# Splitting a chunk's outputs over two visits of a recurrence chain, with its value transposes in the chain's own bank

## The chip, the cores and the metric

The kernel runs on one core of one Trainium2 chip. The metric is the device time of one execution in microseconds; the time before is the median of three runs.

## The reference, cut to what matters

One layer of a hybrid block on 512 tokens with 16 learned tokens in front (528), width 1024, all in float32:

```
u = rmsnorm(h); proj = u @ w_in
y_rw = rwkv7_branch(...)          # 8 heads of 64: S = S (diag(w) + a^T b) + v^T k ; y = S r
                                  # then a group norm per head, a bonus term, and a gate
y_fx = fox_branch(...)            # 8 heads of causal attention with a forget gate
h = h + (gA * (y_rw @ w_out_rw) + gB * (y_fx @ w_out_fx)) @ w_o
z = rmsnorm(h)
h = h + square(relu(z @ w_up)) @ w_down
```

The change touches the recurrence S, the group norm behind it, and the transposes of z.

## The kernel before, in words

**Products.** Big matrix products are made from a rounded part and a remainder of each factor, in three passes (`passes`). Every transpose is a TensorE (PE) instruction against an identity, from SBUF into PSUM, and ACT and DVE copy the result out.

**The recurrence.** The 8 heads form 4 pairs; a pair's two heads lie on partitions 0 to 63 and 64 to 127 (`hss`). Time is cut into 9 chunks of 64 tokens. Two chains (`chain(g, prs)`, g = 0 and 1) carry two pairs each through the chunks. A chunk has three visits, with a `yield` between them at which other work may come in:

1. L1053: products of the rows L with the state and the values `uv[:, 1]`, into part 0 of the bank `pch` (tag `ch`); DVE copies them to `Rs` (L1055).
2. The inverse visit, L1059: the inverse `Tt` times `Rs`, into part 1 of the same bank; two DVE copies (L1061), one for each half of the partitions, make u, `uv[:, 0]`. `new_uv` transposes the next chunk's values (L1039) into a bank of the tag `py`, and ACT copies them out (L1041). ACT also scales the old state (L1071).
3. L1076: the state's update into part 2 of `pch`, added by DVE (L1078). Then the chunk's outputs, from the second chunk on: four products with L (L1084) and four with Bm (L1087), in a bank of the tag `py`, copied out by ACT (L1088).

The tag `py` has one buffer, so that value transposes and outputs take it in turns; the tag `ch` has one too. Each product of float32 stands in the profile as two instructions, so four products are eight.

**The order.** PE's order in this stage is the order in which the program writes its instructions. `Turns.run` writes it: streams of work (the chains at rank 0, the preparation of the chains at 1, attention at 2 and 3, group norm at 4, projections at 8) yield a time at which they can go on, and the planner takes the first by rank whose time, by the planner's own model of the engines (`Clock`), has come. The model knows when tiles are written and when a bank is free for its next tile; it keeps no times for parts of a tile:

```
SLACK = 0.15
HOP = 0.15
RATE = {"DVE": (0.18, 1.06e-3), "Activation": (0.25, 0.85e-3), "Pool": (0.30, 2.1e-3)}
```

Projections (L580) are what is left to fill in; when all else is done the rest of them follows. The orders of ACT, DVE and the queues are made by the framework, and so are all waits between engines.

**Group norm.** `group_norm` takes four chunks of outputs, normalises them, and turns them with eight transposes of 128 rows and 64 columns (L1114), a bank for each pair; ACT copies them out (L1122) and DVE finishes (L1124, L1125). The gate's products are L1117.

**The MLP's rows.** After the merge, `turned(i, xt)` transposes 128 tokens of z: eight transposes of 128 by 128 (L1264) in two banks, each copied out by ACT (L1265) and DVE (L1266). It runs four times, between the groups of products L1274.

Attention does two things that the prediction uses: scores on half the rows each (L738), and transposed weights (L770) in one bank, from which DVE copies some columns (L773) and ACT others (L774). Key transposes are L947.

Of the kernel before, what the change touches and what calls it, by code (L numbers as in the profile page):

```python
# [9 lines left out]
F32 = mybir.dt.float32  # L10
# [4 lines left out]
ALU = mybir.AluOpType  # L15
# [11 lines left out]
KB = 8  # L27
# [160 lines left out]
def kernel(ctx, tc, ht, x, win, par, cst, gain, lora, wout, wo, wup, wdn, out, dbg=None):  # L188
    nc = tc.nc
    dbg = dbg or {}  # L190
    mm = nc.tensor.matmul
    act = nc.scalar.activation
    V, G, A = nc.vector, nc.gpsimd, nc.scalar
# [12 lines left out]
    ident, ones_blk, tmask, cmask = (cs[:, 128 * i:128 * i + 128] for i in range(4))  # L206
# [74 lines left out]
    ps = ctx.enter_context(tc.tile_pool(name="ps", bufs=2, space=PSUM))  # L281
# [4 lines left out]
    with ExitStack() as st:  # L286
# [5 lines left out]
        def psm(name="psm"):  # L292
            return ps.tile([128, 512], F32, name=name, tag="sm", bufs=4)
# [23 lines left out]
        ck = Clock(nc)  # L317
# [9 lines left out]
        with tc.tile_pool(name="xp", bufs=2) as xp:  # L327
            ones = xp.tile([128, 128], F32, name="ones", bufs=1)
            V.memset(ones, 1.0)
            xt = [yp.tile([128, KB, HT], F32, name=f"xt{t}", tag=("y_rw", "y_fx")[t]) for t in range(2)]  # L330
# [30 lines left out]
            def rest(i):  # L361
                V.tensor_tensor(olo[i], raws[i], ohi[i].bitcast(F32), ALU.subtract)
# [142 lines left out]
        turns = Turns(tc, ck)  # L505
        hss = [slice(0, 64), slice(64, 128)]
# [299 lines left out]
        def v9(t):  # L806
            return t.rearrange("p (a b) -> p a b", b=64)
# [218 lines left out]
        def chain(g, prs):  # L1026

            y = y_rw[:, 2 * g:2 * g + 2, :].rearrange("p a (b c) -> p a b c", c=64)
            lws = [load_lora(2 * g + pr_, 1, 2) for pr_ in range(2)]

            def ppy(name):
                return ps.tile([128, 512], F32, name=name, tag="py", bufs=1)

            def new_uv(c):

                uv = rp.tile([128, 2, 2, 2, 64], F32, name="uv", bufs=2)
                pv = ppy("pvt").rearrange("p (a b) -> p a b", b=128)
                for pr_ in range(2):
                    nc.tensor.transpose(pv[:64, pr_, :], prs[pr_].ov[:, 64 * c:64 * c + 64], ident)  # L1039
                for e in range(2):  # L1040
                    A.copy(uv[hss[1 - e], :, e, :, :], bc(pv[:64, :2, 64 * e:64 * e + 64], 1, 2))  # L1041
                return uv

            yield lambda: math.inf if lent else max(ck.ready(Tt, prs[1].bkT), ck.ring("py", 1, 1))
            uv = new_uv(0)
            for e, hs in enumerate(hss):
                V.memset(uv[hs, 1, e, :, :], 0.0)
            for c in range(NCH):
                yield lambda: max(ck.ready(uv), ck.ring("ch", 1, 1) if c == 0 else 0.0)
                ch = ps.tile([128, 512], F32, name="pch", tag="ch", bufs=1)[:, :384].rearrange("p (a b c) -> p a b c", b=2, c=64)  # L1050
                for pr_ in range(2):
                    for e, hs in enumerate(hss):
                        mm(ch[hs, 0, pr_, :], prs[pr_].L[e][:, c, :64], uv[:, 1, e, pr_, :], start=True, stop=True)  # L1053
                Rs = rp.tile([128, 2, 64], F32, name="Rs")
                V.tensor_copy(Rs, ch[:, 0])  # L1055
                yield lambda: ck.ready(Rs)
                for pr_ in range(2):
                    for hs in hss:
                        mm(ch[hs, 1, pr_, :], Tt[hs, pr_, c, :], Rs[hs, pr_], start=True, stop=True)  # L1059
                for e, hs in enumerate(hss):  # L1060
                    V.tensor_copy(uv[hs, 0, e], ch[hs, 1])  # L1061
                if c < NCH - 1:
                    nxt = new_uv(c + 1)
                    if c == NCH - 2:
                        values_read[g].done = True
                        if g == 0:
                            seconds[0].ask_values()
                    SP = rp.tile([128, 2, 64], F32, name="SP")
                    for e, hs in enumerate(hss):
                        for pr_ in range(2):  # L1070
                            act(SP[hs, pr_], uv[hs, 1, e, pr_], AF.Copy, scale=prs[pr_].pend[hs, c:c + 1])  # L1071
                yield lambda: max(ck.ready(uv), ck.ring("py", 1, 1))
                if c < NCH - 1:
                    for pr_ in range(2):
                        for e, hs in enumerate(hss):
                            mm(ch[hs, 2, pr_, :], prs[pr_].bkT[:, c, 64 * e:64 * e + 64], uv[:, 0, e, pr_, :], start=True, stop=True)  # L1076
                    for e, hs in enumerate(hss):
                        V.tensor_tensor(nxt[hs, 1, e], ch[hs, 2], SP[hs], ALU.add)  # L1078
                if c > 0:

                    py = v9(ppy("pyy"))
                    for pr_ in range(2):
                        for e, hs in enumerate(hss):
                            mm(py[hs, pr_, :], prs[pr_].L[e][:, c, 64:128], uv[:, 1, e, pr_, :], start=pr_ == 0, stop=False)  # L1084
                    for pr_ in range(2):
                        for e, hs in enumerate(hss):
                            mm(py[hs, pr_, :], prs[pr_].Bm[hs, c, 64:128], uv[hs, 0, e, pr_, :], start=False, stop=pr_ == 1)  # L1087
                    A.copy(y[:, :, c - 1, :], py[:, :2, :])  # L1088
                if c in (4, 8):
                    turns.add(4, group_norm(g, y[:, :, c - 4:c, :], c - 4, prs, lws))  # L1090
                if c < NCH - 1:
                    uv = nxt
            chained[g].done = True
            chains[0] -= 1

        def group_norm(g, y, c0, prs, lws):

            st1 = rp.tile([128, 2, 4], F32, name="st1")
            V.tensor_reduce(st1, y, AX.X, ALU.add)
            V.tensor_scalar(st1, st1, 1.0 / 64, None, ALU.mult)  # L1100
            V.tensor_tensor(y, y, bc(st1, 3, 64), ALU.subtract)
            ysq = rp.tile([128, 2, 4, 64], F32, name="ysq", tag="Ain")
            act(ysq, y, AF.Square)
            st2 = rp.tile([128, 2, 4], F32, name="st2")
            V.tensor_reduce(st2, ysq, AX.X, ALU.add)
            V.tensor_scalar(st2, st2, 1.0 / 64, 64e-5, ALU.mult, ALU.add)
            rs = rsqrt(st2, rp, "rsg", [128, 2, 4])
            V.tensor_tensor(y, y, bc(rs, 3, 64), ALU.mult)
            yield lambda: max(ck.ready(y_rw), banks(3))
            pts = [psm("pyt").rearrange("p (a b) -> p a b", b=128) for pr_ in range(2)]  # L1110
            pos = psm("pg").rearrange("p (a b) -> p a b", b=256)
            for pr_ in range(2):
                for i in range(4):
                    nc.tensor.transpose(pts[pr_][:64, i, :], y[:, pr_, i, :], ident)  # L1114
            for pr_ in range(2):
                for n, (a, b) in enumerate(passes(lws[pr_], [x[:, 1, NM + 64 * c0:NM + 64 * c0 + 256] for x in (lhi, llo)])):
                    mm(pos[:, pr_, :], a, b, start=n == 0, stop=n == 2)  # L1117
            for pr_ in range(2):
                p = 2 * g + pr_
                yT = rp.tile([128, 4, 64], F32, name="yT", bufs=1)  # L1120
                for e, hs in enumerate(hss):
                    A.copy(yT[hs], pts[pr_][:64, :, 64 * e:64 * e + 64])  # L1122
                yf = yT.rearrange("p a b -> p (a b)")
                V.scalar_tensor_tensor(yf, yf, pr[:, C_LG + p:C_LG + p + 1], prs[pr_].bv[:, 64 * c0:64 * c0 + 256], ALU.mult, ALU.add)  # L1124
                V.tensor_tensor(y_rw[:, p, 64 * c0:64 * c0 + 256], yf, pos[:, pr_, :], ALU.mult)  # L1125
            normalised[g][c0 // 4].done = True
# [64 lines left out]
    def ppd():  # L1191
        tag = ("pj", "pj", "ch", "py")[wide[0] % 4]
        wide[0] += 1
        return ps.tile([128, 512], F32, name="pd", tag=tag, bufs=2 if tag == "pj" else 1)

    with ExitStack() as st:
# [42 lines left out]
        for b2 in range(4):  # L1239
            w = load_w(wo[0, b2])  # L1240
            for i, b1 in [(i, b1) for b1 in range(2) for i in range(4)] if b2 < 3 else [(i, b1) for i in range(4) for b1 in range(2)]:
                k = 2 * b2 + b1
# [13 lines left out]
            act(xt[:, :512], hr, AF.Square, accum_out=ssb[:, i:i + 1])  # L1256
            V.tensor_scalar(ssb[:, i:i + 1], ssb[:, i:i + 1], 1.0 / 1024, 1e-6, ALU.mult, ALU.add)
        def turned(i, xt):
            tk = slice(128 * i, 128 * i + 128)
            for j in range(2):  # L1260
                kk = slice(4 * j, 4 * j + 4)
                pt = ppd().rearrange("p (b c) -> p b c", c=128)
                for k in range(4):
                    nc.tensor.transpose(pt[:, k, :], xt[:, 512 * j + 128 * k:512 * j + 128 * k + 128], ident)  # L1264
                A.copy(zhi[:, kk, tk], pt)  # L1265
                V.tensor_tensor(zlo[:, kk, tk], pt, zhi[:, kk, tk].bitcast(F32), ALU.subtract)  # L1266

        normed = []
        for i in range(4):
# [291 lines left out]
```

## Time and profile before

| | us |
|---|---|
| median of three runs | 840.73 (839.65 to 841.92) |
| profiled execution, its own time | 840.95 |
| span of its instructions | 839.2 |
| PE busy / PE weight loads | 826.2 / 679.4 |
| DVE / ACT / POOL busy | 606.9 / 451.9 / 117.8 |
| first chain, from its first product (L1053) to its last inverse product (L1059) | 135.0 to 193.4 |
| second chain, the same | 300.2 to 350.5 |

A row of a timeline begins with the start in us from the span's start and the time from the first start to the last end of the instructions merged in it; then come engine, line, operation, names and shapes. PE matmuls overlap: an instruction lasts longer than its distance from the next. In a shape such as 64\*128, the first number is the rows and the second the columns of the array that the instruction uses. PEld is PE's weight load. In square brackets stands the idle time before an instruction and what ended it. A row of the windows gives the stretch, its length, the busy time and count of PE, PEld, DVE, ACT and POOL, the granted PE clock, and the share and rate of the DMA engines.

### The profile page before, as it was taken

What the parts mean: (1) busy time and instruction counts of PE and PEld (TensorE: products, weight loads), DVE (VectorE), ACT (ScalarE), POOL (GpSimd) and SP (SyncE); (2) the same over time, 40 slices, a digit from 0 to 9 for tenths busy, and PEclk for the clock granted to TensorE, in tenths of its full rate; (3) what the DMA queues carried; (4) which work ended last, traced back from release to release, by engine and by line L of the source; (5) the groups of instructions that cost most, each with busy time, mean ns of one, the idle gap of its engine ahead of it and who ended that gap; (6) DMA issues with size and microseconds to landing.
All of it is one profiled execution on the core that took longest, in us unless ns stands there. A gap on an engine that the chain in (4) does not pass through costs nothing.

```text
span 839.2 us, 15281 instructions
## 1 busy us (share of the span) xinstructions
PE 826.2 (98%) x5758; PEld 679.4 (81%) x5758; DVE 606.9 (72%) x1209; ACT 451.9 (54%) x933; POOL 117.8 (14%) x121
## 2 busy tenths in 40 slices
PE   8999999999999999999999999999999999999998
PEld 6979886686997877687887789888888888888886
DVE  6897976688779665864257644975698569867988
ACT  7767539665754276644357523565445434544452
POOL 1011000001010000000022002100650065007300
PEclk9999999999999999999999999999999999999999
DMA  7231221211112220232588403631753275336531
GB/s 235 73 91 63 65 77 43 65 53 64 54 59 91 89 65 27 76 115 91 186 281 281 140 26 101 201 102 42 255 155 101 74 229 160 90 108 209 160 102 75
DMA packets 51482, 95.88 MB, mean 114 GB/s; under 512 B 5832, under 2 KB 7240, under 8 KB 51408
## 3 DMA queue, kind: packets, MB, share of 16 engines
q1 hardware_dynamic: 47680, 86.38, 32.6%
q0 software_dynamic: 1280, 4.20, 1.7%
q10 hardware_dynamic: 2448, 4.33, 1.5%
q8 instruction: 45, 0.74, 0.4%
q14 instruction: 29, 0.24, 0.1%
HBM read 88.57 MB, written 6.31 MB: 113 GB/s over the span
## 4 chain that ended last, share of the span: by engine, by line
PE 84%; DVE 6%; ACT 4%; DMA 3%; issue 2%; POOL 1%; SPq 0%; DVEq 0%; ACTq 0%; POOLq 0%
PE pj L580 24%; PE po L1302 21%; PE po L1429 12%; PE pd L1429 5%; PE po L1274 3%; PE pw L993 2%; PE psc L738 1%; PE pj L395 1%; DMA gl<-gd 1%; PE py L786 1%; PE ppt L770 1%; PE pch L1059 1%; PE po L1244 1%; PE pd L1244 1%; DVE wlo L550 1%
## 5 line engine op out<-in xcount | busy, mean ns | idle before, releaser
L580 PE MATMUL pj<-uhi,whi 128*128 128x264 f32 (+1 forms) x480 | 164.8, 343 | 0.0
L580 PE MATMUL pj<-ulo,whi 128*128 128x264 f32 (+1 forms) x480 | 154.1, 321 | 0.0
L580 PE MATMUL pj<-uhi,wlo 128*128 128x264 f32 (+1 forms) x480 | 154.0, 321 | 0.0
L239 DVE TENSOR_TENSOR wlo<-wraw,whi 128x512 fp32r<-128x512 f32 x84 | 78.6, 947 | 40.2 <-ACT whi L238 40.0
L580 PEld LDWEIGHTS pj<-uhi,whi 128*128 128x128 f32 x480 | 90.2, 188 | 14.5 <-issue 6.1
L580 PEld LDWEIGHTS pj<-ulo,whi 128*128 128x128 f32 x480 | 90.4, 188 | 7.7 <-issue 2.4
L580 PEld LDWEIGHTS pj<-uhi,wlo 128*128 128x128 f32 x480 | 90.3, 188 | 6.9
L1302 PE MATMUL po<-zhi,whi 128*128 128x512 f32 (+1 forms) x248 | 94.8, 382 | 0.0
L1302 PE MATMUL po<-zlo,whi 128*128 128x512 f32 (+1 forms) x248 | 94.8, 382 | 0.0
L1302 PE MATMUL po<-zhi,wlo 128*128 128x512 f32 (+1 forms) x248 | 94.8, 382 | 0.0
L238 ACT CAST whi<-wraw 128x512 fp32r<-128x512 f32 x84 | 51.5, 618 | 58.7 <-PE po L1302 19.5
L549 ACT CAST whi<-wraw 128x512 fp32r<-128x512 f32 x78 | 47.6, 617 | 43.1 <-PE pj L580 40.7
L550 DVE TENSOR_TENSOR wlo<-wraw,whi 128x512 fp32r<-128x512 f32 x78 | 52.7, 685 | 21.8 <-ACT whi L549 19.2
L273 ACT CAST whi<-t 128x512 fp32r<-128x512 f32 x64 | 39.9, 624 | 44.5 <-DVE wlo L274 27.2
L1429 PE MATMUL po<-wlo,fhi 128*128 128x512 f32 (+1 forms) x164 | 63.4, 387 | 0.1
L1429 PE MATMUL po<-whi,flo 128*128 128x512 f32 (+1 forms) x164 | 62.9, 384 | 0.0
L1429 PE MATMUL po<-whi,fhi 128*128 128x512 f32 (+1 forms) x164 | 62.3, 384 | 0.0
L1351 POOL TENSOR_TENSOR t<-traw 128x512 f32<-128x512 f32 x24 | 37.1, 1561 | 173.5 <-DMA traw<-in_wdn 121.3
L274 DVE TENSOR_TENSOR wlo<-t,whi 128x512 fp32r<-128x512 f32 x64 | 43.6, 689 | 24.3 <-ACT whi L273 24.1
L1318 ACT CAST fhi<-R 128x768 fp32r<-128x768 f32 (+1 forms) x32 | 30.2, 944 | 46.1 <-DVE R L1325 25.1
L1302 PEld LDWEIGHTS po<-zlo,whi 128*128 128x128 f32 x248 | 46.6, 188 | 9.1
L1302 PEld LDWEIGHTS po<-zhi,whi 128*128 128x128 f32 x248 | 46.6, 188 | 9.0
(316 smaller groups left out, 1741.4 us busy)
## 6 DMA issues: line engine op xcount, KB each, us to landing
wraw<-in_win SPq DMA_DIRECT2D x84, 256.0 KB, 2.6
wraw<-in_wup SPq DMA_DIRECT2D x60, 256.0 KB, 3.1
wraw<-in_wdn SPq DMA_DIRECT2D x48, 256.0 KB, 2.7
traw<-in_wdn SPq DMA_DIRECT2D x48, 256.0 KB, 3.6
gd<-gt ACTq DMA_DIRECT2D x16, 256.0 KB, 2.5
wraw<-in_wout SPq DMA_DIRECT2D x16, 256.0 KB, 3.9
gl<-gd SPq DMA_DIRECT2D x16, 256.0 KB, 3.6
traw<-in_wdn POOLq DMA_DIRECT2D x16, 256.0 KB, 3.2
```

The source lines that it names most:

```text
L238: A.copy(hi, raw)
L239: low.tensor_tensor(lo, raw, hi.bitcast(F32), ALU.subtract)
L273: A.copy(hi, x)
L274: V.tensor_tensor(lo, x, hi.bitcast(F32), ALU.subtract)
L549: after(A.copy(hi, raw), last["ACT"])
L550: after(V.tensor_tensor(lo, raw, hi.bitcast(F32), ALU.subtract), last["DVE"])
L580: mm(po, a, b[:, k, a0:a1], start=n == 0, stop=n == 23)
L1274: mm(po, a[:, k, 128 * i:128 * i + 128], b[:, k, :], start=n == 0, stop=n == 23)
L1302: mm(po[:, t0:t1], a, b[:, k, t0:t1], start=n == 0, stop=n == 23)
L1318: A.copy(fhi[:, j, a:b], R[:, a:b])
L1351: eng.tensor_tensor(t, sums[c, pair] if c in (T1, T2) else c, d, ALU.add)
L1429: mm(x[i][:, cols], a[:, k, left, 128 * rows:128 * rows + 128], c[:, cols], start=start and k == 0 and n == 0, stop=stop and k == n_pairs ...
```

## The change

- A chunk's products with L (L1084) stay in the third visit. Its products with Bm and the copy of the outputs (`rest`) move to the next chunk's inverse visit, behind the inverse's products and before the value transposes; the last chunk's get a visit of their own. The group norms are added from there.
- The next chunk's values are transposed into the chain's bank, in columns 0 to 127 and 384 to 511, which part 0 no longer needs and the chain doesn't use. The first chunk's still go to a bank of the tag `py`.
- Group norm: sixteen transposes of 64 by 64 in place of eight, the halves of the partitions in turn, a bank for each half.
- MLP rows: sixteen transposes of 64 rows and 128 columns in place of eight, halves in turn, a bank for each half of the tokens; the copies read both banks after all of them.

```diff
-            def new_uv(c):
+            def new_uv(c, pv):
 
                 uv = rp.tile([128, 2, 2, 2, 64], F32, name="uv", bufs=2)
-                pv = ppy("pvt").rearrange("p (a b) -> p a b", b=128)
                 for pr_ in range(2):
                     nc.tensor.transpose(pv[:64, pr_, :], prs[pr_].ov[:, 64 * c:64 * c + 64], ident)
...
-            uv = new_uv(0)
+            uv = new_uv(0, ppy("pvt")[:, :256].rearrange("p (a b) -> p a b", b=128))
...
+            def outputs(c, uv):
+
+                py = v9(ppy("pyy"))
+                for pr_ in range(2):
+                    for e, hs in enumerate(hss):
+                        mm(py[hs, pr_, :], prs[pr_].L[e][:, c, 64:128], uv[:, 1, e, pr_, :], start=pr_ == 0, stop=False)
+
+                def rest():
+                    for pr_ in range(2):
+                        for e, hs in enumerate(hss):
+                            mm(py[hs, pr_, :], prs[pr_].Bm[hs, c, 64:128], uv[hs, 0, e, pr_, :], start=False, stop=pr_ == 1)
+                    A.copy(y[:, :, c - 1, :], py[:, :2, :])
+                    if c in (4, 8):
+                        turns.add(4, group_norm(g, y[:, :, c - 4:c, :], c - 4, prs, lws))
+                return rest
+
+            rest = None
             for c in range(NCH):
...
-                ch = ps.tile([128, 512], F32, name="pch", tag="ch", bufs=1)[:, :384].rearrange("p (a b c) -> p a b c", b=2, c=64)
+                bank = ps.tile([128, 512], F32, name="pch", tag="ch", bufs=1)
+                ch = bank[:, :384].rearrange("p (a b c) -> p a b c", b=2, c=64)
...
                 for e, hs in enumerate(hss):
                     V.tensor_copy(uv[hs, 0, e], ch[hs, 1])
+                if rest:
+                    rest()
                 if c < NCH - 1:
-                    nxt = new_uv(c + 1)
+                    nxt = new_uv(c + 1, bank.rearrange("p (a b) -> p a b", b=128)[:, 0:4:3, :])
...
                 if c > 0:
-
-                    py = v9(ppy("pyy"))
...
-                if c in (4, 8):
-                    turns.add(4, group_norm(g, y[:, :, c - 4:c, :], c - 4, prs, lws))
+                    rest = outputs(c, uv)
                 if c < NCH - 1:
                     uv = nxt
+            yield lambda: ck.ready(uv)
+            rest()
             chained[g].done = True
...
-            pts = [psm("pyt").rearrange("p (a b) -> p a b", b=128) for pr_ in range(2)]
+            pts = [v9(psm("pyt")) for e in range(2)]
...
-                    nc.tensor.transpose(pts[pr_][:64, i, :], y[:, pr_, i, :], ident)
+                    for e, hs in enumerate(hss):
+                        nc.tensor.transpose(pts[e][:64, 4 * pr_ + i, :], y[hs, pr_, i, :], ident[hs, hs])
...
-            tk = slice(128 * i, 128 * i + 128)
-            for j in range(2):
-                kk = slice(4 * j, 4 * j + 4)
-                pt = ppd().rearrange("p (b c) -> p b c", c=128)
-                for k in range(4):
-                    nc.tensor.transpose(pt[:, k, :], xt[:, 512 * j + 128 * k:512 * j + 128 * k + 128], ident)
-                A.copy(zhi[:, kk, tk], pt)
-                V.tensor_tensor(zlo[:, kk, tk], pt, zhi[:, kk, tk].bitcast(F32), ALU.subtract)
+            pts = [ppd().rearrange("p (b c) -> p b c", c=64) for j in range(2)]
+            for k in range(KB):
+                for pt, hs in zip(pts, hss):
+                    nc.tensor.transpose(pt[:, k, :], xt[hs, 128 * k:128 * k + 128], ident[hs, hs])
+            for j, pt in enumerate(pts):
+                tk = slice(128 * i + 64 * j, 128 * i + 64 * j + 64)
+                A.copy(zhi[:, :, tk], pt)
+                V.tensor_tensor(zlo[:, :, tk], pt, zhi[:, :, tk].bitcast(F32), ALU.subtract)
```

More of the change, by code (lines that the diff above doesn't have):

```diff
@@ L1079, in chain @@
                 if c > 0:
-                    py = v9(ppy("pyy"))
[L1082 to L1088, printed above, removed]
-                if c in (4, 8):
-                    turns.add(4, group_norm(g, y[:, :, c - 4:c, :], c - 4, prs, lws))
+                    rest = outputs(c, uv)
                 if c < NCH - 1:
                     uv = nxt
+            yield lambda: ck.ready(uv)
+            rest()
             chained[g].done = True
@@ L1121, in group_norm @@
                 for e, hs in enumerate(hss):
-                    A.copy(yT[hs], pts[pr_][:64, :, 64 * e:64 * e + 64])
+                    A.copy(yT[hs], pts[e][:64, 4 * pr_:4 * pr_ + 4, :])
                 yf = yT.rearrange("p a b -> p (a b)")
```

## The prediction

> **What bounds the kernel now.** I read the engine shares first, then the busy time by stretch, then the chain that ended last, and then the timeline of one chunk.
>
> ```profile
> span 839.2 us, 15281 instructions
> PE 826.2 (98%) x5758; PEld 679.4 (81%) x5758; DVE 606.9 (72%) x1209; ACT 451.9 (54%) x933; POOL 117.8 (14%) x121
> ...
> 130.00:195.00 65.00, 63.99 (x649) 49.13 (x646) 48.34 (x169) 48.73 (x137) 1.96 (x4) 1.00 0.19 59
> 298.00:357.00 59.00, 58.37 (x588) 43.10 (x587) 40.10 (x137) 40.01 (x116) 0.00 (x0) 1.00 0.18 56
> 385.50:413.00 27.50, 27.50 (x121) 22.29 (x120) 9.16 (x15) 9.91 (x18) 0.00 (x0) 1.00 0.42 136
> ...
> 385.52 27.57 PE pj L580 x119
> ```
>
> PE is busy for 98% of the span, at the full granted clock (1.00). The two chains run at 130 to 195 and at 298 to 357 us; there PE is without work for only 1.01 + 0.63 us. The last piece, from the chain's list, is what decides how a saving or a loss counts: after the second chain and its group norms, 27.57 us of projections (L580) are still left, and PE does them without a gap. Everything before 413 us competes for one PE. A microsecond less on PE in the chains ends that filler a microsecond earlier, and a microsecond in which PE stands at a wait, with its hand-written order behind it, ends it a microsecond later. How early the chain itself ends is worth nothing.
>
> So each part is costed by the time it takes from PE. One chunk, the second of the first chain, looks so (PE, the copies, and at the end the first projections again):
>
> ```profile
> 143.35 0.45 PE L1059 MATMUL pch<-Rs,Tt 64*64 64x64 f32 x8
> 143.73 0.41 PE L1039 MATMUL pvt<-cs,ov 128*64 128x128 f32 x2
> 143.84 0.59 DVE L1061 COPY uv<-pch 64x128 f32<-64x128 f32 x2
> 144.17 0.74 ACT L1041 COPY uv<-pvt 64x256 f32<-64x256 f32 x2 [0.21 <-PE pvt L1039]
> 146.75 0.45 PE L1076 MATMUL pch<-uv,bkT 128*64 128x64 f32 x8
> 147.03 0.40 PE L1084 MATMUL pyy<-uv,L 128*64 128x64 f32 x8
> 147.36 0.45 PE L1087 MATMUL pyy<-uv,Bm 64*64 64x64 f32 x8
> 147.74 0.39 PE L580 MATMUL pj<-uhi,whi 128*128 128x264 f32 x1
> 147.86 0.27 ACT L1088 COPY y_rw<-pyy 128x128 f32<-128x128 f32 x1 [0.74 <-PE pyy L1087]
> 147.97 0.28 PE L580 MATMUL pj<-ulo,whi 128*128 128x264 f32 x1
> 148.09 0.28 PE L580 MATMUL pj<-uhi,wlo 128*128 128x264 f32 x1
> ...
> L1059 PE MATMUL pch<-Rs,Tt x144: 218/218/268, 135.9 to 350.8; 64*64 64x64 f32 x144
> L1084 PE MATMUL pyy<-uv,L x128: 222/222/270, 147.0 to 353.4; 128*64 128x64 f32 x128
> L1061 DVE COPY uv<-pch x36: 257/289/295, 137.1 to 351.3; 64x128 f32<-64x128 f32 x36
> ```
>
> The inverse visit is L1059 with the transposes L1039 right behind it; the third visit is L1076, L1084 and L1087. The last three rows are of the views by line: least, median and longest duration in ns.
>
> **Part 1, the moved products: a gain of 2.1 us.** Eight instructions of L1084 take 0.40 us from first start to last end; the last lasts 0.22 (last rows, medians by line), so the last starts at 147.03 + 0.40 - 0.22 = 147.21, and they run as pairs 0.06 us apart. L1087 should follow at 147.27 and starts at 147.36: going from 128*64 to 64*64 costs 0.09 us, and its own eight take 0.05 us longer than L1084's. That is 0.15 us per change of shape. In the changed kernel Bm's products follow L1059, which has the same 64*64 shape, and this change of shape is gone. It happens for chunks 1 to 7 of both chains, 14 times: 14 x 0.15 = 2.1 us. Chunk 8's products still come in a visit of their own, as before. The bounds are 0.09 x 14 = 1.3 and 2.1; I take 2.1. The copy L1088 (0.27) moves with them and stays beside PE. The group norms start one visit later, which the 27.57 us of filler behind the last of them hide. Nothing that moves issues a DMA.
>
> **Part 2, the values in the chain's bank: a loss of 6.3 us.** Today L1039 writes a bank of its own and follows L1059 without a wait (143.35 + 0.45 - 0.22 = 143.58 is L1059's last start; 143.73 is 0.15 later). In the changed kernel it writes the bank from whose middle DVE is still copying u (L1061). The columns differ, but do columns decide? Attention has this case: of one bank, DVE copies some columns (L773) and ACT others (L774).
>
> ```profile
> 138.85 0.29 DVE L773 COPY pT<-ppt 128x128 f32<-128x128 f32 x1
> 139.13 0.28 DVE L773 COPY pT<-ppt 128x128 f32<-128x128 f32 x1
> 139.19 0.52 ACT L774 COPY pTm<-ppt 16x128 f32<-16x128 f32 x2
> ...
> who waited for it (us, times):
>   ACT pTm L774: 8.2, 8
> ```
>
> ACT starts 0.05 us after DVE's first copy has ended (138.85 + 0.29 = 139.14, 139.19), and eight times it waited for L773, 8.2 us in all, though the two have no value in common. So accesses to one bank are put one behind the other, and the transposes will wait for DVE. They write partitions 0 to 63, which they share with the first L1061 copy alone; the row shows a wait between instructions that share partitions, so I take the first copy and leave the second as a rival. That copy ends at 143.84 + 0.29 (L1061's median) = 144.13; with 0.05 for the handover PE may go on at 144.18. PE is free at 143.73, or, with Bm's four pairs (0.24) in front, at 143.97. It stands 0.21 us with the cover and 0.45 without. The cover is there where the chunk before has outputs, in chunks 2 to 7 of each chain (12 times); chunks 0 and 1 have none (4 times): 12 x 0.21 + 4 x 0.45 = 4.3 us. That is with DVE free. It is late in places, as in the first of these sixteen chunks and a little in the last:
>
> ```profile
> 135.94 0.45 PE L1059 MATMUL pch<-Rs,Tt 64*64 64x64 f32 x8
> 137.07 0.56 DVE L1061 COPY uv<-pch 64x128 f32<-64x128 f32 x2
> ...
> 345.01 0.45 PE L1059 MATMUL pch<-Rs,Tt 64*64 64x64 f32 x8
> 345.51 0.59 DVE L1061 COPY uv<-pch 64x128 f32<-64x128 f32 x2
> ```
>
> 137.07 is 1.13 after L1059 began, 0.64 more than the 0.49 of the sample chunk; 345.51 is 0.50 after. The excess over the sixteen rows of this kind sums to 2.0 us. Today projections run meanwhile; with the transposes next in PE's order nothing does. 4.3 + 2.0 = 6.3 us. Queued behind the waiting transposes on PE are all the projections and attention; ACT's copies L1041 come as much later, and ACT, in order too, holds what follows.
>
> **Part 3, the third visit: a loss of 2.5 us.** L1076 writes the same bank, so it must wait for ACT's two copies L1041, which end 144.17 + 0.74 - 143.73 = 1.18 us after the transposes began. Today the planner waits for them, because they free the output bank; after the change that bank is freed by L1088, and the planner asks only for L1061 and L1088. By the rates in its code (DVE 0.18 + 128 x 0.00106 = 0.32 per u copy, ACT 0.25 + 256 x 0.00085 = 0.47 per value copy) two u copies after L1059 replace the transposes (0.31) and two value copies behind them, and with their handovers it can put the visit some 0.6 us sooner. PE needs 1.18 + 0.05 - 0.25 (its own two transposes) = 0.98 us of other work in between. The planner's smallest piece of projections is six, 0.12 apart (147.97, 148.09), so 0.72: one leaves 0.26, two leave nothing. Sixteen visits at the short piece are 4.2 us, none is 0; I take 2.5, rather over the middle because ACT's copies come late where DVE's do.
>
> **Part 4, the transposes in halves: a gain of 0.5 us.** Today's transposes take 0.11 us each, bound by 128 moving columns:
>
> ```profile
> 492.02 1.03 PE L1264 MATMUL pd<-cs,xt 128*128 128x128 f32 x8
> 492.81 0.48 PE L1274 MATMUL po<-wohi,mhi 128*128 128x512 f32 x1
> 493.12 0.40 PE L1274 MATMUL po<-wolo,mhi 128*128 128x512 f32 x1
> ...
> L738 PE MATMUL psc<-ka,qa x80: 282/389/601, 123.0 to 354.7; 64*128 64x272 f32 x32, 64*128 64x144 f32 x16, 64*128 64x400 f32 x16, 64*128 64x256 f32 x16
> 127.17 0.73 PE L738 MATMUL psc<-ka,qa 64*128 64x272 f32 x4
> ...
> 90.74 0.20 PEld L947 LDWEIGHTS pbt<-cs,KT 128*128 128x128 f32 x2 [0.17 <-issue]
> ...
> 147.74 0.19 PEld L580 LDWEIGHTS pj<-uhi,whi 128*128 128x128 f32 x1
> 147.85 0.19 PEld L580 LDWEIGHTS pj<-ulo,whi 128*128 128x128 f32 x1
> ```
>
> Eight take 8 x 0.11 = 0.87 us, with no loss at either edge. Sixteen halves stream 64 columns each. L738 shows that two row halves run side by side: four instructions take 0.73 us, where a single one lasts 0.39 at the median. So a visit is eight pairs at the 0.06 us of the 64-column pairs above, 0.47 us. Into it goes a change of shape (0.09, and about 0.04 for the first weights), and out another: L580 after L1087 starts 0.09 late (147.74 for 147.65), and its second instruction comes 0.23 later, not 0.12: 0.20 together. 0.47 + 0.33 = 0.80, a gain of 0.07 per visit; four group norm visits and four MLP visits, 8 x 0.07 = 0.5 us. If halves didn't pair, a visit would take 8 x 0.11 + 0.33 and lose 0.33, 2.7 us in all. That is the other end. The evacuations keep their sizes; both banks of an MLP visit are read after all sixteen, hidden by the 6 us of L1274 until the next visit.
>
> A half's weights must also load in 0.06 us. L947's two loads of 128 columns start 0.06 apart (0.20 together, 0.14 each), where two ordinary ones (147.74, 147.85) are 0.11 apart. [...]
>
> **The sum.** The 1.64 us in which PE waits in the chains today will partly fall into the new waits, as DVE and ACT catch up meanwhile: -0.8, half of them. 840.95 - 2.1 + 6.3 + 2.5 - 0.5 - 0.8 = 846.35 for the profiled execution (its span is 839.2, the rest lies around it). It is 0.22 above the median of the three runs, 840.73, so I say 846.2 us, 0.6% slower. I call 0.3%, 2.5 us, what a measurement of this kernel can just tell from no change.
>
> **The rivals.**
> - *Both copies.* The transposes wait for the whole bank, so for the second L1061 copy too: 0.30 us more in each of sixteen chunks, 4.8 us, 851.0. For it: L774 waits although no column is shared. Against: no row shows a wait between different partitions. [...]
> - *The other side: the transposes need not wait at all.* If only overlapping columns bind, parts 2 and 3 fall away: 840.95 - 2.1 - 0.5 is 838.35, 838.1 against the median. For it: the columns are disjoint. Against: L774. It decides when L1039 starts within 0.1 us of Bm's last product.
> - *The wait lies under the cover.* DVE free in every chunk (4.3), nothing in part 3: 840.95 - 2.1 + 4.3 - 0.5 - 0.8 = 841.85, 841.6, no change that can be told. For it: in nine of sixteen chunks DVE is on time today. Against: DVE's load in the chains, 48.34 of 65 and 40.10 of 59 us.
> - *All of it.* Both copies, 4.2 in part 3 and halves that don't pair: 851.0 + 1.7 + 3.2 = 855.9.
>
> **How the numbers follow.** The forecast has 0.40, both copies 0.25, all of it 0.08: slower 0.73. Under the cover has 0.13: same. No wait has 0.14: faster. The range is 841 to 854: it leaves out the no-wait case and nearly all of the worst. The likeliest case alone would be 844 to 849.
>
> **What would show it.** In the changed kernel: L1087's line right behind L1059's without 0.09 us between them; the transposes' idle time put down to DVE's u copy, some 0.2 us where Bm's products stand in front and 0.45 where not; PE idle in the two chain stretches grown from 1.64 to some 9 us; L1076's wait put down to ACT's value copies; group norm and MLP transposes as sixteen in about 0.6 us to the last end. The prediction is wrong if the transposes start at once, if they wait until the second copy has ended, or if the planner, whose order rests on these costs, fills the chains in another way so that the third visit waits long.

## The result: 850.15 us, 1.2% slower

| | before | after |
|---|---|---|
| median, us | 840.73 (839.65 to 841.92) | 850.15 (849.37 to 852.47), five runs |
| profiled execution / its span, us | 840.95 / 839.2 | 849.37 / 847.6 |
| PE without work in the two chain stretches, us | 1.64 | 13.79 |
| last of the projections L580 ends, us | 413.3 | 422.2 |

The ratio is 1.0117 [1.0104, 1.0130]. The direction and the range held; the point, 846.2, is 4 us too low.

The lines have moved. The chain's first products are L1070 (L1053 before), the copy to `Rs` L1072 (L1055), the inverse products L1076 (L1059), the u copies L1078 (L1061), the third visit L1095 (L1076); the value transposes are L1038 (L1039), their copies on ACT L1040 (L1041); the products with L and Bm are L1052 and L1057 (L1084, L1087), the copy of the outputs L1058 (L1088).

The page's totals of the kernel after, the windows of the two chains and of the end of the projections, and that piece from the chain that ended last:

```profile
span 847.6 us, 15420 instructions
PE 820.6 (97%) x5822; PEld 672.8 (79%) x5822; DVE 609.5 (72%) x1209; ACT 452.8 (53%) x933; POOL 117.4 (14%) x121
...
130.00:195.00 65.00, 58.10 (x604) 43.33 (x602) 43.80 (x151) 46.17 (x128) 1.76 (x4) 1.00 0.16 50
316.00:383.00 67.00, 60.11 (x565) 41.28 (x562) 42.72 (x143) 36.96 (x109) 0.00 (x0) 1.00 0.20 64
410.50:422.50 12.00, 12.00 (x53) 9.75 (x52) 5.58 (x10) 5.89 (x11) 0.00 (x0) 1.00 0.39 128
...
410.42 11.61 PE pj L580 x50
```

PE's busy time has fallen and the span has grown. In the chains PE stands for 65.00 - 58.10 and 67.00 - 60.11 us. The filler is still there at the end, 11.61 us of it without a gap: PE remains the only thing that bounds this half, and what it lost at waits came out as time. The waits of PE from 120 to 420 us (line, what it waited for, us in all, times, longest):

```profile
PE pch L1038 <- DVE uv L1078: 10.5, 16, 1.3
PE py L783 <- ACT pTm L774: 1.8, 1, 1.8
PE pup L869 <- ACT sg L258: 0.8, 1, 0.8
PE pch L1095 <- ACT uv L1040: 0.8, 3, 0.3
PE pch L1076 <- DVE tm L305: 0.7, 1, 0.7
PE pch L1076 <- DVE Rs L1072: 0.6, 1, 0.6
```

One line holds most of it: the transposes in the chain's bank wait for DVE's u copies in all sixteen chunks. A chunk with Bm's products in front, and one without:

```profile
152.96 0.45 PE L1076 MATMUL pch<-Rs,Tt 64*64 64x64 f32 x8
153.24 0.40 PE L1057 MATMUL pyy<-uv,Bm 64*64 64x64 f32 x8
153.46 0.58 DVE L1078 COPY uv<-pch 64x128 f32<-64x128 f32 x2
154.10 0.41 PE L1038 MATMUL pch<-cs,ov 128*64 128x128 f32 x2 [0.46 <-DVE uv L1078]
154.54 0.74 ACT L1040 COPY uv<-pch 64x256 f32<-64x256 f32 x2 [0.59 <-PE pch L1038]
155.34 0.45 PE L1095 MATMUL pch<-uv,bkT 128*64 128x64 f32 x8
...
144.31 0.45 PE L1076 MATMUL pch<-Rs,Tt 64*64 64x64 f32 x8
144.81 0.59 DVE L1078 COPY uv<-pch 64x128 f32<-64x128 f32 x2 [0.17 <-PE pch L1076]
145.45 0.41 PE L1038 MATMUL pch<-cs,ov 128*64 128x128 f32 x2 [0.69 <-DVE uv L1078]
```

The DVE row holds both copies. They end at 153.46 + 0.58 = 154.04 and 144.81 + 0.59 = 145.40, and the transposes start 0.06 and 0.05 us later. So they waited for the *second* copy. In DVE's order that is the copy of partitions 64 to 127, which the transposes don't write. From the start of the last inverse product (152.96 + 0.45 - 0.22 = 153.19, and 144.54) it is 0.91 us in both; before it was 0.15. Bm's products shorten the wait from 0.69 to 0.46 and don't remove it.

### The profile page after: what moved, and what is told of

Read it like the earlier page. It is cut to its first block, busy times and chain, and to the rows that moved or that the text cites. A ratio compares the mean times of both kernels' runs of the same rounds, so it can differ in the third digit from the quotient of the medians.

```text
span 847.6 us, 15420 instructions
## 1 busy us (share of the span) xinstructions
PE 820.6 (97%) x5822; PEld 672.8 (79%) x5822; DVE 609.5 (72%) x1209; ACT 452.8 (53%) x933; POOL 117.4 (14%) x121
## 4 chain that ended last, share of the span: by engine, by line
PE 51%; DVE 3%; DMA 3%; ACT 1%; issue 1%; POOL 1%; SPq 0%; DVEq 0%; ACTq 0%; POOLq 0%
PE po L1314 20%; PE po L1441 12%; PE pj L580 6%; PE pd L1441 5%; PE po L1286 3%; DMA gl<-gd 2%; PE po L1256 1%; PE pd L1256 1%; DVE wlo L239 1%; PE py L786 1%; POOL gl L1229 1%; DMA zhiraw<-in_wo 0%; DMA gd<-gt 0%; DMA wraw<-in_wo 0%; DVE gl L1227 0%
## 5 line engine op out<-in xcount | busy, mean ns | idle before, releaser
L580 PE MATMUL pj<-uhi,whi 128*128 128x264 f32 (+1 forms) x480 | 164.5, 343 | 0.0
L580 PE MATMUL pj<-ulo,whi 128*128 128x264 f32 (+1 forms) x480 | 154.1, 321 | 0.0
L580 PE MATMUL pj<-uhi,wlo 128*128 128x264 f32 (+1 forms) x480 | 154.0, 321 | 0.0
L239 DVE TENSOR_TENSOR wlo<-wraw,whi 128x512 fp32r<-128x512 f32 x84 | 81.8, 984 | 38.5 <-ACT whi L238 38.5
L580 PEld LDWEIGHTS pj<-uhi,whi 128*128 128x128 f32 x480 | 90.2, 188 | 12.3 <-issue 4.4
L580 PEld LDWEIGHTS pj<-ulo,whi 128*128 128x128 f32 x480 | 90.4, 188 | 7.5 <-issue 2.4
L580 PEld LDWEIGHTS pj<-uhi,wlo 128*128 128x128 f32 x480 | 90.3, 188 | 6.9
L550 DVE TENSOR_TENSOR wlo<-wraw,whi 128x512 fp32r<-128x512 f32 x78 | 52.9, 686 | 16.2 <-ACT whi L549 14.8
L1314 PEld LDWEIGHTS po<-zhi,wlo 128*128 128x128 f32 x248 | 46.6, 188 | 9.0
```

What stands on the lines that cost most here:

```text
L239: low.tensor_tensor(lo, raw, hi.bitcast(F32), ALU.subtract)
L550: after(V.tensor_tensor(lo, raw, hi.bitcast(F32), ALU.subtract), last["DVE"])
L580: mm(po, a, b[:, k, a0:a1], start=n == 0, stop=n == 23)
L1314: mm(po[:, t0:t1], a, b[:, k, t0:t1], start=n == 0, stop=n == 23)
```

## The experiments

The theory (W in the expectations, B in e5's): DVE's copies and the transposes share a bank, the bank as a whole binds, and this wait is the loss. Its rivals: only the copy of the shared partitions binds, and DVE happens to make it second (Q); the loss lies in the order that the planner now makes, with a second chain that starts at 316.7 us and not at 300.2 (P); the halves or the moved products cost more than they seem. The kernel before ran beside each group at 840.8 to 841.0 us; ratios are to it.

**e1, the halves alone.** The kernel before with only the edits in `group_norm` and `turned`.

> The kernel before with only the transposes in halves (group norm and MLP rows); the chains as before. Theory W (the loss is PE's wait at the value transposes, which stand in the chain's bank): no wait is added here, and by the prediction's part 4 the eight visits gain 0.07 us each, so 840.7 - 0.5 = 840.2 us, not to be told from before. Rival H (the halves lose, because row halves do not pair or the changes of shape cost more than 0.33 us a visit): up to 843.4. A visit's sixteen transposes should stand 0.06 us per pair apart by W, 0.11 or more by H.

Measured: 840.11 us, 0.9987 [0.9976, 0.9998]. A group norm visit in its timeline (L1115 are the transposes, L1118 the gate's products):

```profile
219.03 0.28 PE L580 MATMUL pj<-uhi,wlo 128*128 128x264 f32 x1
219.25 0.64 PE L1115 MATMUL pyt<-cs,y_rw 64*64 64x64 f32 x16
219.81 0.39 PE L1118 MATMUL pg<-lhi,lw 128*128 128x256 f32 x1
220.04 0.28 PE L1118 MATMUL pg<-llo,lw 128*128 128x256 f32 x1
```

Sixteen transposes take 0.64 us, and 0.64 - 0.22 for the last one leaves 0.42 for fifteen starts: pairs 0.06 us apart, as forecast. From 219.03 to 220.04 is 1.01 us, two ordinary steps of 0.12 among it: the visit costs PE 0.77 us with its edges, where eight whole transposes and theirs took 0.87. So halves run in pairs, and H falls. Not every visit gains, though. The fourth MLP visit (L1263 in this kernel) stands in PE's order as two groups, with products between:

```profile
507.06 0.28 PE L1303 MATMUL po<-zlo,we 128*128 128x256 f32 x1
507.54 0.46 PE L1263 MATMUL pd<-cs,xt 64*128 64x64 f32 x8 [0.20 <-DVE xt L1287]
507.93 0.51 PE L1303 MATMUL po<-zhi,we 128*128 128x256 f32 x2
508.37 0.46 PE L1263 MATMUL pd<-cs,xt 64*128 64x64 f32 x8
```

It changes shape four times and not twice. From the product in front to the third one behind it takes 2.05 us (507.06 to 509.10), where the kernel before, split in the same way, took 1.72 (508.20 to 509.92).

**e2, all but the halves.** The change with `group_norm` and `turned` as before.

> The changed kernel with the whole transposes of before in group norm and MLP; only the chain's two edits are left. Theory W: the wait of PE for DVE's u copies, 10.5 us in the changed kernel's trace, stays, so 850.2 + 0.5 = 850.7 us. Rival H: what the halves lose comes back, 847. The two edits of the change should add up: this run's difference to before and the halves' difference should sum to 9.4 us.

Measured: 852.13 us, 1.0125 [1.0110, 1.0141]; PE's wait at L1038 is the same 10.5 us in 16. The whole loss lies in the chain's two edits, and this run and e1 add up to the change: +1.25% - 0.13% = 1.12%, against 1.17%.

**e3, the values in a bank of their own.** The change, with the transposes in a bank that group norm and the preparation share, and the inverse visit asking for a free one:

```diff
-                yield lambda: ck.ready(Rs)
+                yield lambda: max(ck.ready(Rs), banks(1))
...
-                    nxt = new_uv(c + 1, bank.rearrange("p (a b) -> p a b", b=128)[:, 0:4:3, :])
+                    nxt = new_uv(c + 1, psm("pvt")[:, :256].rearrange("p (a b) -> p a b", b=128))
```

> The changed kernel, but the next chunk's values are transposed into one of the four banks that attention and the others share (tag sm), and the inverse visit also asks the planner for such a bank; the moved products stay. Theory W: the 10.5 us wait of the transposes and the waits of the third visit for ACT's value copies go, and the gains of parts 1 and 4 stay: 838 to 840.5 us, PE idle in the chains back under 3 us. Rival P (the loss is in the order that the planner makes with the moved products: the second chain starts at 317 us in place of 300): the order stays about as it is, 847 to 850. In between if the shared banks are short: waits of PE at attention's banks, up to 845.

Measured: 837.74 us, 0.9967 [0.9953, 0.9980]: faster than either kernel, a little under the range expected, and near the 838.1 that the prediction gives for no wait. Its windows of the chains, and its second chunk:

```profile
130.00:195.00 65.00, 64.12 (x654) 49.56 (x651) 47.97 (x149) 47.35 (x128) 3.48 (x8) 1.00 0.18 57
309.00:370.00 61.00, 60.24 (x559) 42.19 (x555) 42.48 (x144) 38.09 (x111) 0.00 (x0) 1.00 0.23 75
...
148.57 0.45 PE L1076 MATMUL pch<-Rs,Tt 64*64 64x64 f32 x8
148.85 0.40 PE L1057 MATMUL pyy<-uv,Bm 64*64 64x64 f32 x8
149.06 0.59 DVE L1078 COPY uv<-pch 64x128 f32<-64x128 f32 x2 [0.79 <-PE pch L1076]
149.18 0.41 PE L1038 MATMUL pvt<-cs,ov 128*64 128x128 f32 x2
```

The transposes start while DVE copies: 0.38 us after the last inverse product (148.57 + 0.23 = 148.80), Bm's 0.24 among it. PE stands 0.88 + 0.76 us in the chains, as before the change. Everything else of the change is in this kernel, a late second chain (309.7 us) too: the other bank alone makes 850.15 - 837.74 = 12.4 us. So P falls as the main cause, and e7 below bears it out: there the second chain starts at 322.5 us, later than in the change, and the time is 842.25.

**e5, the u copies in the other order.** One run, for Q; in DVE's order the copies of partitions 64 to 127 now come first, in all eighteen chunks. If only shared partitions bound, then of the two orders one would let the transposes go a copy (0.3 us) earlier.

```diff
-                for e, hs in enumerate(hss):
+                for e, hs in list(enumerate(hss))[::-1]:
                     V.tensor_copy(uv[hs, 0, e], ch[hs, 1])
```

> The changed kernel with DVE's two u copies asked for in the other order (partitions 64 to 127 first, then 0 to 63). Theory B (the whole bank binds, whichever partitions): the transposes go on 0.05 us after the later of the two copies, 0.91 us after the last inverse product where DVE is free, as in the changed kernel. Rival Q (only shared partitions bind, and in the changed kernel the copy of partitions 0 to 63 happened to run second): now it runs first, and the transposes start 0.60 after. Time by B 850, by Q about 845.

```profile
159.06 0.45 PE L1076 MATMUL pch<-Rs,Tt 64*64 64x64 f32 x8
159.34 0.40 PE L1057 MATMUL pyy<-uv,Bm 64*64 64x64 f32 x8
159.56 0.59 DVE L1078 COPY uv<-pch 64x128 f32<-64x128 f32 x2 [0.99 <-PE pch L1076]
160.20 0.41 PE L1038 MATMUL pch<-cs,ov 128*64 128x128 f32 x2 [0.46 <-DVE uv L1078]
```

The transposes again start 0.91 us after the last inverse product (159.29) and 0.05 after the second copy's end (160.15). The wait is 11.2 us in 16. Q falls: whichever half is copied last, the transposes wait until then. (Its time, 854.02 us, is a single run.)

**e6, no cover.** The transposes ahead of `rest()`, so that Bm's products never stand between.

> The changed kernel with the moved products behind the value transposes, not ahead of them. Theory W: nothing covers the wait now, so the twelve transposes that had the products in front wait 0.24 us longer, 2.9 us, and the products must change from the transposes' shape back to 64*64, some 0.14 each for fourteen, 2 us: 850.2 + 4.9 = 855. Rival P (the order decides, not the wait): 850.

Measured: 854.92 us, 1.0179 [1.0156, 1.0202], as the theory has it (855).

```profile
PE pch L1038 <- DVE uv L1078: 12.8, 16, 1.3
```

The wait grows by 12.8 - 10.5 = 2.3 us for twelve covered chunks of 0.24 us (2.9); the medians stand 4.8 us apart, and the rest was not taken apart.

**e4, the transposes ahead of the inverse products.** At that place DVE has no copy from the bank to make.

```diff
                 yield lambda: ck.ready(Rs)
+                if c < NCH - 1:
+                    pv = turn(c + 1, bank.rearrange("p (a b) -> p a b", b=128)[:, 0:4:3, :])
...
-                    nxt = new_uv(c + 1, bank.rearrange("p (a b) -> p a b", b=128)[:, 0:4:3, :])
+                    nxt = new_uv(pv)
```

> The changed kernel with the value transposes still in the chain's bank, but issued ahead of the inverse products, when the bank has no reader left; ACT's copies stay behind DVE's u copies. Theory W: PE waits no more for the u copies at the transposes; ACT's copies then end 0.4 us earlier after the inverse products, so that the third visit's wait shrinks too; against it the exit from the 64*64 shape costs some 0.1 us more, 16 times: 840.7 - 2.1 - 0.5 + 1.6 = 839.7, range 838.5 to 842. Rival P: 847 to 850. Rival S (same place, other wait: the transposes or the inverse products now wait for DVE's Rs copy or for ACT): the wait shows at the inverse products and the time stays over 845.

Measured: 847.51 us, 1.0070 [1.0057, 1.0084], a miss: what came is rival S. In this kernel the third visit is L1100, the value copies are L1043, the transposes L1036, the copy to `Rs` L1075, the inverse products L1081, the u copies L1083. Its largest waits of PE, and a chunk:

```profile
PE pch L1100 <- ACT uv L1043: 3.7, 5, 1.2
PE pch L1036 <- DVE Rs L1075: 3.3, 2, 1.9
...
158.73 0.45 PE L1081 MATMUL pch<-Rs,Tt 64*64 64x64 f32 x8
159.23 0.59 DVE L1083 COPY uv<-pch 64x128 f32<-64x128 f32 x2 [0.48 <-PE pch L1081]
160.00 0.74 ACT L1043 COPY uv<-pch 64x256 f32<-64x256 f32 x2
160.79 0.45 PE L1100 MATMUL pch<-uv,bkT 128*64 128x64 f32 x8 [0.74 <-ACT uv L1043]
```

The wait for DVE's u copies is gone, and the one of part 3 is there, 3.7 us in five visits: the third visit starts 160.79 - 160.74 = 0.05 us after ACT's second value copy, which the planner doesn't ask for. The two don't overlap in the bank either: ACT reads columns 0 to 127 and 384 to 511, and the third visit writes 256 to 383. The 3.3 us for `Rs` are not of this kind, since the inverse products right behind need `Rs` too. I had let the wait go and not asked what is late next.

**e9 and e10, the planner asks for the values.** One edit, on the change (e9) and on e4 (e10):

```diff
-                yield lambda: max(ck.ready(uv), ck.ring("py", 1, 1))
+                yield lambda: max(ck.ready(uv, nxt), ck.ring("py", 1, 1))
```

> The changed kernel, but the third visit's stop also asks the planner for the next chunk's values, which ACT copies out of the bank (the missing condition of the prediction's part 3). Theory W: the wait at the transposes, 10.5 us, stays; only what the third visit waited for ACT goes, 1 to 3 us: 847 to 849. Rival R (the planner's ignorance is the larger part of the loss): below 845.

> The kernel with the transposes ahead of the inverse products, which came to 847.5 us, with the third visit asking for the next values too. In its trace PE's third visit waited for ACT's value copies, one bank behind DVE's u copies. If that is why that run missed its forecast, other work now fills the third visit's waits: 4 to 6 us less, 842 to 843.5. If the wait of the transposes for DVE's Rs copy, 3.3 us, is the larger part: 846 to 847.

e9: 851.24 us, 1.0113 [1.0095, 1.0131], no gain and a miss. e10: 843.9 us, 1.0030 [1.0017, 1.0043], 0.4 over its range and far from the other one (846 to 847). Their waits, e9 first, then e10:

```profile
PE pch L1038 <- DVE uv L1078: 10.7, 16, 1.3
PE pch L1076 <- DVE Rs L1072: 2.4, 4, 1.5
```

```profile
PE pch L1036 <- DVE Rs L1075: 4.4, 4, 1.8
PE pch L1100 <- ACT uv L1043: 1.3, 3, 0.7
```

In e9 ACT's copies no longer hold the third visit, and PE's time is not better: in the change the third visit's wait was only 0.8 us, and 2.4 us of waiting for `Rs`, 0.6 before this edit, take its place. In e10 the same line is worth 0.40% between the ratios, 3.4 us, because there the wait was large. What is left in e10 is mostly the wait for `Rs`. The inverse products need its values in any order (PE waited 0.8 us for it in the kernel before), so this is not the bank's doing.

**e7, a stop between the copies and the transposes.** The change with one more visit, in which the planner may put other work, and with e9's edit, which was worth nothing by itself:

```diff
                 if c < NCH - 1:
+                    yield lambda: ck.ready(uv)
                     nxt = new_uv(c + 1, bank.rearrange("p (a b) -> p a b", b=128)[:, 0:4:3, :])
...
-                yield lambda: max(ck.ready(uv), ck.ring("py", 1, 1))
+                yield lambda: max(ck.ready(uv, nxt), ck.ring("py", 1, 1))
```

> The changed kernel with a further stop of the chain between the moved products and the value transposes, at which the planner may put other work until DVE's u copies should be done, and with the third visit asking for the value copies too. The transposes stay in the chain's bank. Theory W: the wait of 10.5 us is filled for the most part, as are the third visit's; each of sixteen stops costs one more exit from the 64*64 shape, some 0.1 us: 850.2 - 11.3 + 1.6 = 840.5, up to 844 where DVE is later than the planner thinks. Rival P: 847 to 850.

Measured: 842.25 us, 1.0018 [1.0008, 1.0029]. No wait for L1078 is left; the largest of PE's from 120 to 420 us is now one in the preparation, and the transposes follow long after the copies:

```profile
PE psr L940 <- DVE Bm L941: 0.9, 2, 0.7
...
152.06 0.58 DVE L1078 COPY uv<-pch 64x128 f32<-64x128 f32 x2
153.95 0.38 PE L1038 MATMUL pch<-cs,ov 128*64 128x128 f32 x2
```

The bank is still shared: here the wait costs nothing that shows, because PE's written order has other work in its place. This gives back 7.9 of the 12.4 us; the rest was not taken apart.

**e8, e3 without the moved products.** The kernel before with the halves and the values in e3's bank; Bm's products stay in the third visit.

> The kernel before with the halves and with the next chunk's values transposed into a shared bank (tag sm), as in the run with the values in a bank of their own; the products with Bm stay in the third visit. It differs from that run by the move alone. By the prediction's part 1 the move gains 2.1 us (14 changes of shape of 0.15), so 837.7 + 2.1 = 839.8 us. Rival: the gain of the run with the values in a bank of their own came from the bank (the transposes no longer wait their turn with the outputs) and not from the move: 837.7 here too. Rival: the move is worth nothing and the order made the difference: anything from 836 to 842.

Measured: 840.44 us, 0.9993 [0.9979, 1.0007]. Against e3 the move alone is worth 0.9993 - 0.9967 = 0.26%, 2.2 us; the two intervals overlap a little, but the traces say the same (part 1 below). e3's gain is part 1 and part 4, and the other bank by itself is worth nothing that can be told.

## Why the prediction was right in sign and short in size

The range held because it had been drawn wide enough for the rival, and the point came as near as it did partly by luck: part 2 was too low by 4 to 5 us, and part 3 too high by 1.7. What fell is one sentence of part 2: "I take the first copy and leave the second as a rival." All sixteen waits ended with the second copy. The rival *both copies* had this at 4.8 us more, 851.0; 850.15 was measured. The forecast had read in L774 that accesses to one bank are put one behind the other, though no value is shared, and then took the narrower reading, by partitions, for which no row spoke. Nothing in the profile of before separated the two; the trace of the change and e5 do. Columns and partitions were both of no help: sixteen of sixteen transposes that write partitions 0 to 63 waited for a copy of 64 to 127, and began 0.05 or 0.06 us after its end. The waits between engines are the framework's, so what these runs show is its rule; whether the chip would have let them go is not tried, since no run lets the two run at once in one bank.

Term by term, from the two profiled executions (840.95 to 849.37, +8.4 us; the prediction's own sum, 846.35 less 0.22, is 846.1 and not 846.2). I summed, for each product on PE up to the last L580, the time from its start to the next start on PE, so that a wait falls to the work in front of it:

| | forecast | inverse products + Bm | value transposes |
|---|---|---|---|
| before | | 6.82 + 6.06 = 12.88 | 4.26 |
| e3, no shared bank | part 1: -2.1 | 5.46 + 5.39 = 10.85 | 3.31 |
| after | part 2: +6.3 | 9.22 + 13.24 = 22.46 | 3.74 |

- **Part 1** (2.1): 12.88 - 10.85 = 2.0 in e3's trace. In e8, which lacks only the move, the same two sum to 6.90 + 6.05 = 12.95, so 2.1, and the medians of e8 and e3 say 2.2. Right.
- **Part 2** (6.3): 22.46 - 10.85 = 11.6, or 10.5 by the list of waits. It was forecast at a wait of 0.21 us with the cover and 0.45 without; the chunks above have 0.46 and 0.69, a second copy more in each of sixteen. This is the missing 4 to 5 us.
- **Part 3** (2.5): the mechanism is there (L1095 waits for ACT's copies), with 0.8 us in three visits. In the first chunk above it starts 155.34 - 155.28 = 0.06 us after ACT's second copy, but attention's transposes fill most of the time until then. Too high here; e4 shows 3.7 us where the first wait is gone.
- **Part 4** (-0.5): in e1 the four group norm visits gain 0.44 us together and three MLP visits 0.11 (0.84 each, against 0.875). The fourth MLP visit loses 2.05 - 1.72 = 0.33: its two groups pay the changes of shape twice, which the prediction counted once, and some of it may be the wait for `xt` in front of them, which was not taken apart. That leaves 0.2: the pairing is right and the sum too high. e1's time, 0.13% [0.02, 0.24] or 1.1 us, can't tell 0.2 from 0.5. The prediction also read loads of L580 0.11 us apart as the pace of loads; their products are 0.12 apart, so that row doesn't say which of the two sets it.
- **The waits elsewhere** (-0.8): the value transposes' own steps gained 0.5, the time after the last L580 0.5, the group norm transposes 0.5; so the rest of PE's work up to there took 8.4 - (22.46 - 12.88) + 1.5 = 0.3 us more. In it L783's 1.8 and the clock's 1.7 (last section) stand against less time elsewhere, 1.5 us of it at the preparation's L940. Of the waits of before, L940's 0.4 us is off the list, the one for `Rs` is 0.6 and was 0.8, and L869's 0.8 has stayed, so they shrank less than forecast; that new ones would come was not foreseen.

The MLP rows of the kernel after:

```profile
500.00 0.39 PE L1286 MATMUL po<-wohi,mlo 128*128 128x512 f32 x1
500.31 0.71 PE L1274 MATMUL pd<-cs,xt 64*128 64x64 f32 x16
500.96 0.50 PE L1286 MATMUL po<-wohi,mhi 128*128 128x512 f32 x1
501.29 0.39 PE L1286 MATMUL po<-wolo,mhi 128*128 128x512 f32 x1
```

Sixteen halves, each with weights of 128 columns, take 500.96 - 500.31 = 0.65 us, their exit among it. Eight pairs at the prediction's 0.06 us (0.47) and its exit of 0.20 make 0.67, so loading these weights held no pair up.

Of the signs listed in advance, L1057's line is right behind L1076's without the change of shape, the halves take some 0.6 us, and the third visit waits for ACT. The idle time in the chains is 13.79 us, not 9. "If they wait until the second copy has ended" was named as what would make the prediction wrong, and that is what happened.

## What to carry to other kernels

With waits as this framework makes them, a PSUM bank that DVE was reading was one lock to PE's writes in these runs, whatever the columns and partitions (sixteen of sixteen, 10.5 us): put a result that is wanted during a read into another bank (e3), or let other work be written between (e7). Price such a wait at the end of the last access to the bank, and then ask which reader of the same bank is late next. On an engine that is the bound and runs in written order, a wait is time (10.5 us of it here, in a loss of 12.4 against e3), and a cover is worth about its own length (0.23 us off the wait for 0.24 of products).

## What the runs showed of the hardware

A part of the loss is clock. In the profile after, PE stood 1.81 us at L783, and 2.0 us after its work went on, from 233.1 to 236.5 us, the granted clock was 0.50. In the slightly wider window below it is 0.54 as a mean over 3.70 us (the entry after POOL's):

```profile
231.07 1.07 PE L783 MATMUL py<-pTm,vm 16*64 16x512 f32 x4 [1.81 <-ACT pTm L774]
...
232.90:236.60 3.70, 3.70 (x31) 1.95 (x27) 0.77 (x1) 0.58 (x1) 0.00 (x0) 0.54 0.00 0
```

It costs PE some 0.46 x 3.70 = 1.7 us. Of 53 runs of the kernel before beside the experiments, 49 have a mean granted clock of 0.999 or more (median 840.8 us) and four 0.997 or 0.998 (843.2). Of e3's twelve, four have 0.997 (840.1, against 837.4 for the others). After the change all five have 0.996 to 0.998. So by this estimate some 2 us of the 9.4 go with the clock, and most runs of the kernels with many waits have such a lower mean (all of e2's five and e4's six, four of e10's six). What sets a stretch off stays open, and no run shows that the waits do: five of e1's twelve have 0.997 or 0.998 without more waits, three of e9's five have 1.000, in a kernel whose trace has waits as long as the change's, and two of e6's four, with the longest waits of all, have 0.999 and 1.000.
